# A hybrid decoder step on one core: level products in 32-column parts, pair products by head, the states' decay on ScalarE

## The chip, the cores and the metric

The kernel runs on one core of one Trainium2 chip. The metric is device time in microseconds of one execution. A core has TensorE (PE: matrix products, with weight loads shown as PEld), VectorE (DVE), ScalarE (ACT), GpSimd (POOL) and SyncE (SP, which issues the transfers). They run side by side and wait for each other through semaphores; each takes its own instructions in order.

## What is computed

One layer of a hybrid decoder for two groups: a prompt of 256 new tokens, and 8 samples of 8 tokens each that carry states from before (320 columns of tokens together).

```python
h = rms_norm(x, norm_g)
p = einsum('nld,dp->nlp', h, w_in)                  # 2048 -> 12416 columns
# branch A, RWKV-7: 16 heads of 64
S_t = S_{t-1} diag(w_t) - (S_{t-1} kk_t)(kk_t * a_t)^T + v_t k_t^T;   y_t = S_t r_t
# branch B, HGRN2: 8 heads of 128
S_t = diag(g_t) S_{t-1} + k_t v_t^T;   o_t = S_t^T q_t
merged = sigmoid(ga) * (y_a @ proj_a) + sigmoid(gb) * (o_b @ proj_b)
y = x + merged @ w_out                              # then a final rms_norm
```

The outputs are `y` of both groups, the end states of both branches, and the last projected row. Everything is in float32.

## The kernel before

**Stages.** A start normalises the tokens and turns them. The main loop follows: eight rounds `p`, each with eight projections of 128 columns of `w_in` (r, k, v, za, q, f, i, zb), then `rwkv(p)` for two heads of branch A (stacked on the 128 partitions, 64 each) and `hgrn(p)` for one head of branch B. Four projections of the gate close the loop. The rest (gates, `proj_a`, `proj_b`, `w_out`, the last norm) is untouched by the change.

**Projections.** Values are kept as a high and a low part; a projection is 48 products of 128 x 128 weights with 320 columns (`mps<-hhi,whi`, `mps<-hlo,whi`, `mps<-hhi,wlo`). Weights arrive as 512 KB pieces (`raw`); ScalarE rounds them to `whi`, VectorE takes the difference as `wlo`. There are three buffers of each.

**Order.** `record_all` doesn't issue the loop's instructions; a `Recorder` (`book`) keeps each as an `Op` with its engine, a cost in ns, and the tiles it reads and writes. `link` finds which Op waits for which, `order` simulates the engines and writes out one fixed order for all of them. So every instruction of the loop has the same line, 1396, and is told by its tiles: `a`, `b` and `y` are accumulators (PSUM) of the two branches. On TensorE small products are put between projections; those on a part of the array (a weight of at most 64 columns or rows) are preferred together, since a change of partition is charged, and those of `hgrn` may wait up to `WAIT` = 6000 ns for company. Small products are given a margin of 250 ns after their inputs.

**RWKV of the prompt** goes by four chunks of 64 tokens; block 4 is the samples. `bk2[:, ci]` has two kinds of columns (64 each) with both heads on the partitions, and `arp[:, ci]` holds the two heads apart, with zeros where the other head is, so one product of 128 rows and 256 columns gives both heads' pair products (`a<-arp,bk`, accumulator `pg`), which VectorE masks into `g2`. The chunk chain (`chunks`: `rhs`, `uv`, `st`, `sf`) then runs from chunk to chunk over TensorE, ScalarE and VectorE.

**RWKV of the samples.** The end states are one product per head, `uv` (64 columns) with `bm`, 64 key columns masked for each of the eight samples, 512 columns (`pd2`; tiles `big` and `s0t`). GpSimd makes the masks' products.

**HGRN.** The prompt's attention inside 128 tokens is built in levels. `level(sz)` scales keys and queries for blocks of `sz`, and a product of 128 x 128 keys and queries gives all pairs, of which a mask (`mu8`) keeps the blocks that belong to the level: levels 0 (`k0`, `q0`) and 8 in one bank, 16, 32 and 64 in another, later one. The samples' own pairs are a product of 64 x 64. `pos` multiplies the samples' states with their queries in eight products of 32 columns. The states decay by one multiplication of 1024 columns on GpSimd (`s0`, `dec`), then two products are added.

Of the kernel before, what the change touches and what calls it, by code (L numbers as in the profile page):

```python
# [11 lines left out]
U8 = mybir.dt.uint8  # L12
# [36 lines left out]
class Op:  # L49
    __slots__ = ("eng", "fn", "args", "kw", "cost", "lat", "uses", "mode", "passes", "cols", "stream",  # L50
                 "succ", "npred", "ready", "rank", "block", "margin", "wait", "port", "hold", "dma", "n")
# [17 lines left out]
class Recorder:  # L69
# [3 lines left out]
    def __init__(self, engines, is_big):  # L73
        self.real, self.ops, self.spans, self.is_big = engines, [], {}, is_big
        self.block, self.wait = None, 0
# [9 lines left out]
    def add(self, eng, name, fn, args, kw):  # L85
# [19 lines left out]
        o.block = self.block  # L105
# [5 lines left out]
        if eng == "PE":  # L111
# [13 lines left out]
            o.cost = o.passes * max(load, stream / min(2, 128 // o.mode[1]))  # L125
# [28 lines left out]
    def link(self):  # L154

        writers, readers = {}, {}
        for o in self.ops:
            o.succ, pred = [], {}
            for name, p0, p1, m, wr, psum in o.uses:
# [22 lines left out]
            o.npred = len(pred)  # L182
            for q, data in pred.values():
# [90 lines left out]
def hybrid_step(ctx, tc, x_prompt, x_sample, state_rwkv, state_hgrn, state_shift, norm_g, w_in,  # L274
# [80 lines left out]
    with tc.tile_pool(name="start", bufs=1) as st, \  # L355
# [83 lines left out]
        seq4 = ctile([96, 4], "seq4")  # L439
# [17 lines left out]
        mf = st.tile([64, 3, 64], F32, name="mf")  # L457
        mu8 = ctile([128, 3, 64], "mu8", U8)
        G.memset(mf, 1.0)
        for n, sz in enumerate((8, 8, 16)):  # L460
            if n == 0:
                mfh = mf[:, 0].rearrange("p (b i) -> p b i", i=8)
                keep_ge(mf[:, 0], [[1, 64]], 0, -1)
                keep_ge(mfh, [[-8, 8], [0, 8]], 0, 1)
                keep_ge(mfh, [[8, 8], [0, 8]], 7, -1)
                continue
            lv = mf[:, n].rearrange("p (b two s) -> p b two s", two=2, s=sz)
            nb = 32 // sz
# [3 lines left out]
        for sl in HS:  # L472
            G.tensor_copy(mu8[sl], mf)
# [49 lines left out]
        with tc.manual_schedule(engines={mybir.EngineType.PE, mybir.EngineType.Activation, mybir.EngineType.DVE,  # L523
# [125 lines left out]
            for j in range(3):  # L649
                S.copy(seq4[32 * j:32 * j + 32], seqm[0:32, 0:4])  # L650
# [34 lines left out]
    def ring(pool, tag, shape, bufs, dt, size, clear=False):  # L685
# [12 lines left out]
        if len(shape) == 2:  # L698
# [5 lines left out]
             "w1": 384, "w2": 320, "w3": 320, "ks": 128, "ket": 256}  # L704


    CLEAR = {"uB", "uE", "ys", "rhs", "rhs2", "k3", "vm", "w1", "vt"}
# [51 lines left out]
    def rwkv(p, r, k, vp, za):  # L759
# [87 lines left out]
        for sp in range(4):  # L847
# [6 lines left out]
        bks = at("bks", (128, 2, 64))  # L854
        V.tensor_mul(bks.rearrange("p j (s i) -> p j s i", i=8), bk2[:, 4].rearrange("p j (s i) -> p j s i", i=8),
                     f[:, None, 8:16, None].to_broadcast([128, 2, 8, 8]))
# [11 lines left out]
        for g in range(3):  # L868
            ps = aps("pg")
            n = 2 if g < 2 else 1  # L870
            for c_ in range(n):
                ci = 2 * g + c_
                T.matmul(ps[:, 256 * c_:256 * c_ + 256], bk2[:, ci].rearrange("p j t -> p (j t)"),
                         arp[:, ci].rearrange("p x h t -> p (x h t)"), start=True, stop=True)
            m = mk[:, 0:2] if g < 2 else mk[:, 2:3]
            V.tensor_mul(g2[:, 2 * g:2 * g + n].rearrange("p c x h t -> p (c x) h t"),
                         ps[:, :256 * n].rearrange("p (a h t) -> p a h t", h=2, t=64),
                         m.rearrange("p c x t -> p (c x) t")[:, :, None].to_broadcast([128, 2 * n, 2, 64]))
# [48 lines left out]
        T.transpose(ps[:, :128], bks.rearrange("p j t -> p (j t)"), ident)  # L927
# [105 lines left out]
        def samples():  # L1033
# [14 lines left out]
            T.matmul(ps[:, :128], g2[:, 4, 0].rearrange("p h t -> p (h t)"), uv[:, 4].rearrange("p h v -> p (h v)"), start=False, stop=True)  # L1048
            rhs = at("rhs2", (128, 2, 64))
# [75 lines left out]
    def hgrn(hd, q, k, v, zb):  # L1125
# [43 lines left out]
        G.memset(att, 0.0)  # L1169

        def level(sz, tag):
            half = lambda t_: t_[:, :NP_].rearrange("p (b two s) -> p b two s", two=2, s=sz)
            kq = bt("kq", (128, NP_), tag=tag)
            if sz in (32, 64):

                side = [kq[:, 128 * x:128 * x + 128].rearrange("p (b s) -> p b s", s=sz) for x in range(2)]
            else:
                side = [half(kq)[:, :, x] for x in range(2)]
# [11 lines left out]

        def products(ps, o_, kq, q_):
            for j in range(2):
                tk_ = slice(128 * j, 128 * j + 128)
                T.matmul(ps[:, o_ + 128 * j:o_ + 128 * j + 128], kq[:, tk_], q_[:, tk_], start=True, stop=True)

        def keep(ps, o_, n):
            own = lambda t_, c_: t_.rearrange("p (j c t) -> p j c t", c=2, t=64)[:, :, c_]
            for c_ in range(2):
                sl = HS[c_]
                V.copy_predicated(own(att[sl, :NP_], c_), mu8[sl, None, n].to_broadcast([64, 2, 64]),  # L1200
                                  own(ps[sl, o_:o_ + NP_], c_))

# [375 lines left out]
```

## Time and profile before

| what | us |
|---|---|
| median of 3 runs | 1157.26 (1156.6 to 1157.67) |
| the profiled execution | 1155.96 |
| its span on the core | 1154.3 |
| TensorE busy | 1135.7 |
| VectorE busy | 775.9 |
| ScalarE busy | 669.2 |
| GpSimd busy | 208.0 |

A group of the profile reads: line, engine, operation, written tile <- read tiles, shapes, count | busy time, mean ns of one | idle time before. The mean of a product is its whole passage, which overlaps the next one's; what one costs TensorE is the distance from start to start, read from the timeline (start, duration, instructions). A view of windows gives a stretch's length, then each engine's busy time and count, the granted clock, and the transfers' share.

### The profile page before, as it was taken

How to read it: one execution, taken by the hardware profiler on the slowest of the kernel's cores; microseconds unless marked ns; L12 is line 12 of the kernel's file. 1: busy time of each engine (PE TensorE's matmuls, PEld its weight loads, DVE VectorE, ACT ScalarE, POOL GpSimd, SP SyncE). 2: the span in 40 equal slices, each digit the busy share in tenths (PEclk: the TensorE clock that was granted, in tenths of full speed). 3: DMA queues.
4: the chain of work that ended last, by engine and by line, in shares of the span. 5: the costliest groups of instructions: out<-in, count | busy, mean ns of one | idle time of the engine just before them, and what ended most of it. 6: DMA issues, size and time to landing. Idle time of an engine off the chain costs nothing.

```text
span 1154.3 us, 20774 instructions
## 1 busy us (share of the span) xinstructions
PE 1135.7 (98%) x7816; PEld 1097.9 (95%) x7816; DVE 775.9 (67%) x1634; ACT 669.2 (58%) x1483; POOL 208.0 (18%) x405
## 2 busy tenths in 40 slices
PE   6999999999999999999999999999999999999997
PEld 6999999999999999999999999999999999998886
DVE  8778878877887888878788686544444444436632
ACT  6766766667666667567667667444444444435322
POOL 9432223222311321421321310000000000000000
PEclk9999999999999999999999999999999999999999
DMA  6745435535445435436435434555555555577512
GB/s 180 199 117 127 129 102 136 142 92 132 129 113 146 117 93 150 131 81 169 120 93 162 115 105 132 148 152 153 152 147 148 151 154 151 146 253 254 182 41 91
DMA packets 283096, 159.69 MB, mean 138 GB/s; under 512 B 22893, under 2 KB 273264, under 8 KB 282356
## 3 DMA queue, kind: packets, MB, share of 16 engines
q1 hardware_dynamic: 282996, 158.37, 48.6%
q8 instruction: 61, 1.00, 0.4%
q14 instruction: 39, 0.32, 0.1%
HBM read 148.53 MB, written 9.81 MB: 137 GB/s over the span
## 4 chain that ended last, share of the span: by engine, by line
PE 96%; POOL 2%; DVE 1%; ACT 1%; issue 0%; DMA 0%; ACTq 0%; POOLq 0%
PE mps L1396 41%; PE a L1396 13%; PE mps L338 6%; PE mps L340 6%; PE mps L339 6%; PE b L1396 4%; PE po L1479 3%; PE po L1481 3%; PE po L1480 3%; PE ppb L338 2%; PE ppa L338 2%; PE ppb L340 2%; PE ppa L340 2%; PE ppa L339 2%; PE ppb L339 2%; PE po L1484 1%
## 5 line engine op out<-in xcount | busy, mean ns | idle before, releaser
L1396 PE MATMUL mps<-hhi,wlo 128*128 128x320 f32 x1088 | 344.9, 317 | 0.0
L1396 PE MATMUL mps<-hlo,whi 128*128 128x320 f32 x1088 | 344.7, 317 | 0.0
L1396 PE MATMUL mps<-hhi,whi 128*128 128x320 f32 x1088 | 344.6, 317 | 0.0
L1396 PEld LDWEIGHTS mps<-hlo,whi 128*128 128x128 f32 x1088 | 204.9, 188 | 3.3 <-issue 3.0
L1396 PEld LDWEIGHTS mps<-hhi,wlo 128*128 128x128 f32 x1088 | 205.0, 188 | 2.7 <-issue 2.4
L1396 PEld LDWEIGHTS mps<-hhi,whi 128*128 128x128 f32 x1088 | 205.0, 188 | 0.8 <-issue 0.4
L329 DVE TENSOR_TENSOR wlo<-raw,whi 128x1024 fp32r<-128x1024 f32 x88 | 107.8, 1225 | 125.0 <-ACT whi L328 124.8
L328 ACT CAST whi<-raw 128x1024 fp32r<-128x1024 f32 x88 | 92.3, 1048 | 163.3 <-PE mps L339 104.8
L1396 ACT CAST whi<-raw 128x1024 fp32r<-128x1024 f32 x134 | 140.6, 1049 | 77.2 <-PE mps L1396 75.8
L1396 DVE TENSOR_TENSOR wlo<-raw,whi 128x1024 fp32r<-128x1024 f32 x134 | 167.5, 1250 | 24.4 <-ACT whi L1396 23.1
L339 PE MATMUL mps<-hlo,whi 128*128 128x320 f32 x448 | 138.5, 309 | 0.0
L338 PE MATMUL mps<-hhi,whi 128*128 128x320 f32 x448 | 138.5, 309 | 0.0
L340 PE MATMUL mps<-hhi,wlo 128*128 128x320 f32 x448 | 138.5, 309 | 0.0
L340 PEld LDWEIGHTS mps<-hhi,wlo 128*128 128x128 f32 x448 | 84.1, 188 | 0.0
L338 PEld LDWEIGHTS mps<-hhi,whi 128*128 128x128 f32 x448 | 84.1, 188 | 0.0
L339 PEld LDWEIGHTS mps<-hlo,whi 128*128 128x128 f32 x448 | 84.1, 188 | 0.0
L1468 DVE TENSOR_TENSOR wlo<-raw,whi 128x1024 fp32r<-128x1024 f32 x32 | 38.5, 1222 | 39.1 <-ACT whi L1467 39.0
L1467 ACT CAST whi<-raw 128x1024 fp32r<-128x1024 f32 x32 | 33.1, 1051 | 48.4 <-DMA raw<-in_w_out_dram 22.4
L1479 PE MATMUL po<-whi,mhi 128*128 128x512 f32 x128 | 50.1, 391 | 0.7 <-DVE gbt L1436 0.7
L1481 PE MATMUL po<-wlo,mhi 128*128 128x512 f32 x128 | 50.0, 391 | 0.0
L1480 PE MATMUL po<-whi,mlo 128*128 128x512 f32 x128 | 50.0, 391 | 0.0
L339 PE MATMUL ppb<-ybl,whi 128*128 128x320 f32 x128 | 39.6, 309 | 0.0
(409 smaller groups left out, 2304.0 us busy)
## 6 DMA issues: line engine op xcount, KB each, us to landing
raw<-in_w_in_dram SPq DMA_DIRECT2D x194, 512.0 KB
raw<-in_w_out_dram SPq DMA_DIRECT2D x32, 512.0 KB
raw<-in_proj_a_dram SPq DMA_DIRECT2D x16, 512.0 KB
raw<-in_proj_b_dram SPq DMA_DIRECT2D x16, 512.0 KB
s<-in_state_hgrn_dram SPq DMA_DIRECT2D x8, 512.0 KB
out_dram<-s SPq DMA_DIRECT2D x8, 512.0 KB
s<-in_state_rwkv_dram SPq DMA_DIRECT2D x8, 256.0 KB
out_dram<-s SPq DMA_DIRECT2D x8, 256.0 KB
```

The source lines that it names most:

```text
L328: S.copy(hi[:, ks], raw[:, ks])
L329: sub.tensor_sub(lo[:, ks], raw[:, ks], hi[:, ks].bitcast(F32))
L338: T.matmul(dst, hi[:, q, :], xhi[:, k, :], start=(k == 0), stop=False)
L339: T.matmul(dst, hi[:, q, :], xlo[:, k, :], start=False, stop=False)
L340: T.matmul(dst, lo[:, q, :], xhi[:, k, :], start=False, stop=(k == nk - 1))
L1396: o.fn(*o.args, **o.kw)
L1467: S.copy(hi, raw)
L1468: V.tensor_sub(lo, raw, hi.bitcast(F32))
L1479: T.matmul(pt, h, hi, start=first, stop=False)
L1480: T.matmul(pt, l, hi, start=False, stop=False)
L1481: T.matmul(pt, h, lo, start=False, stop=end)
L1484: T.matmul(pt, h, hi, start=first, stop=False)
```

## The change

Four edits, and what the planner needs for them.

- *Level products in 32-column parts.* All five levels are computed first. Then `pos`, the products of the levels and the samples' own pairs go out as one group: each key block of 32 tokens is a weight of 32 columns and goes to one of four column parts of the array (`tile32`, part g), with the 32 queries of its own block; level 32 with the 32 queries that follow, level 64 with 64. The results stand in one bank: three masked copies gather the first three levels in `attc` (64 columns), ScalarE spreads them into `att`, VectorE copies the rest. `att` is cleared once at the start and no longer by GpSimd in each head. `kq16`, `kq32`, `kq64` take the buffers of `o`, `ket`, `s1` and `ks`.
- *Pair products by head.* For the four prompt blocks each head's 64 rows are multiplied with that head's 128 columns alone: two products of 64 rows per block, on the upper and lower half of the array's rows, into two banks. The sample block stays as it was.
- *The samples' delta-rule states in four 64 by 64 parts.* `bks` is laid out by halves of the samples, `uh` is `uv` with the samples' halves apart, one masked `bm` serves four samples of each half, and four products of 64 rows, 64 weight columns and 256 columns go to the four quarters of the array, into two banks.
- *Decay on ScalarE.* Eight activations of 128 columns with a scale per partition take the place of the GpSimd multiplication.

`side_by_side` marks products as one group; `link` gives all of a group the waits of each and the highest rank, and the cost of a product in a group is divided by the parts that fit.

```diff
@@ Recorder.add
-            o.cost = o.passes * max(load, stream / min(2, 128 // o.mode[1]))
+            side = 128 // o.mode[1] * (128 // o.mode[0] if o.group else 1)
+            o.cost = o.passes * max(max(load, stream) / side, 7) if o.group else o.passes * max(load, stream / min(2, side))
@@ Recorder.link
+        for members in groups.values():
+            own = {o.n for o in members}
+            shared = {}
+            for o in members:
+                for n, (q, data) in preds[o.n].items():
+                    if n not in own:
+                        shared[n] = q, data or shared.get(n, (q, False))[1]
+            for o in members:
+                preds[o.n].update(shared)
...
+        for members in groups.values():
+            top = max(o.rank for o in members)
+            for o in members:
+                o.rank = top
@@ rwkv
-        for g in range(3):
-            ps = aps("pg")
-            n = 2 if g < 2 else 1
-            for c_ in range(n):
-                ci = 2 * g + c_
-                T.matmul(ps[:, 256 * c_:256 * c_ + 256], bk2[:, ci].rearrange("p j t -> p (j t)"),
-                         arp[:, ci].rearrange("p x h t -> p (x h t)"), start=True, stop=True)
...
+        banks = [aps("pg") for _ in HS]
+        side_by_side([((banks[h][:, 128 * ci:128 * ci + 128], bk2[HS[h], ci].rearrange("p j t -> p (j t)"),
+                        arp[HS[h], ci, :, h]), dict(start=True, stop=True)) for ci in range(4) for h in range(2)])
...
@@ samples
+            uh = at("uh", (128, 128), tag="s0t")
+            for a_ in range(2):
+                S.copy(uh[64 * a_ + 32:64 * a_ + 64], uv[64 + 32 * a_:96 + 32 * a_, 4].rearrange("p h v -> p (h v)"))
...
-            pd = aps("pd2")
-            for h in range(2):
-                bm = at("bm", (128, NSEQ, 64), tag=("big", "s0t")[h])
-                G.tensor_mul(bm, bk[:, 4, None, 64 * h:64 * h + 64].to_broadcast([128, NSEQ, 64]),
-                             seqm[:, :, None].to_broadcast([128, NSEQ, 64]))
-                T.matmul(pd[HS[h], :], uv[:, 4, h, :], bm.rearrange("p s k -> p (s k)"), start=True, stop=True)
-            V.tensor_add(s0, s0, pd.rearrange("p (s k) -> p s k", s=NSEQ))
+            bm = at("bm", (128, 4, 128), tag="big")
+            G.tensor_mul(bm, bk[:, 4, None].to_broadcast([128, 4, 128]), seq4[:, :, None].to_broadcast([128, 4, 128]))
+            pds = [aps("pd2") for _ in HS]
+            side_by_side([((pds[a_][HS[h], :256], uh[HS[a_], 64 * h:64 * h + 64], bm[HS[a_], :, 64 * h:64 * h + 64]),
+                           dict(start=True, stop=True)) for h in range(2) for a_ in range(2)])
+            for a_ in range(2):
+                s0h = s0[:, 4 * a_:4 * a_ + 4]
+                V.tensor_add(s0h, s0h, pds[a_][:, :256].rearrange("p (s k) -> p s k", s=4))
@@ hgrn
-        kq8 = level(8, "w2")
-        ps = bps("pg")
-        products(ps, 0, k0, q0)
-        products(ps, 256, kq8, kq8)
-        keep(ps, 0, 0)
-        keep(ps, 256, 1)
+        kq8, kq16, kq32, kq64 = level(8, "w2"), level(16, "o"), level(32, "ket"), level(64, ("s1", "ks"))
...
+        work = [((ps[32 * j:32 * j + 32, 128 * g:128 * g + 128], qz[:, 4 * g + j], s0[:, 4 * g + j]))
+                for g in range(2) for j in range(4)]
+        tile32 = lambda g, c0, a_, b_: work.append((pg[32 * g:32 * g + 32, c0:c0 + b_.shape[-1]], a_, b_))
+        for n, (a_, b_) in enumerate(((k0, q0), (kq8, kq8), (kq16, kq16))):
+            for j in range(2):
+                for g in range(4):
+                    tk_ = slice(128 * j + 32 * g, 128 * j + 32 * g + 32)
+                    tile32(g, 64 * n + 32 * j, a_[:, tk_], b_[:, tk_])
+        for g in range(4):
+            tile32(g, 192, kq32[0][:, 32 * g:32 * g + 32], kq32[1][:, 32 * g:32 * g + 32])
+        for g in range(4):
+            tile32(g, 224, kq64[0][:, 32 * g:32 * g + 32], kq64[1][:, 64 * (g // 2):64 * (g // 2) + 64])
+        for g in range(2):
+            tk_ = slice(NP_ + 32 * g, NP_ + 32 * g + 32)
+            tile32(g, 288, k0[:, tk_], q0[:, tk_])
+        side_by_side([(x_, dict(start=True, stop=True)) for x_ in work])
+        attc = bt("attc", (128, 2, 32))
+        for n in range(3):
+            V.copy_predicated(attc, mu8[:, None, n].to_broadcast([128, 2, 32]),
+                              pg[:, 64 * n:64 * n + 64].rearrange("p (j t) -> p j t", t=32))
...
-        G.tensor_mul(s0, s0, dec[:, :, None].to_broadcast([128, NSEQ, 128]))
+        for si in range(NSEQ):
+            S.activation(s0[:, si], s0[:, si], AF.Copy, scale=dec[:, si:si + 1])
...
-        kq16, kq32, kq64 = level(16, "w3"), level(32, "w2"), level(64, "w1")
-        ps = bps("pl")
-        products(ps, 0, kq16, kq16)
-        T.matmul(ps[:, 256:384], kq32[:, 0:128], kq32[:, 128:256], start=True, stop=True)
-        T.matmul(ps[:, 384:512], kq64[:, 0:128], kq64[:, 128:256], start=True, stop=True)
...
+    def side_by_side(products):
+        book.group = len(book.ops)
+        for args, kw in products:
+            T.matmul(*args, **kw)
+        book.group = None
```

How the order moves. First TensorE in the first head, where the HGRN products stand (`w_0_...` are the buffers of `kq` and of `k0`, `q0`; `big`, `s0t` those of `bm`, and after the change `s0t` that of `uh`). Before:

```order
L1396 MATMUL b_520<-w_0_525,w_0_517 128x128 x2
...
L1396 MATMUL b_519<-s_0_516,qz 32x128 x8
L1396 MATMUL a_485<-big_514,uv_492 64x512
L1396 MATMUL a_485<-s0t_494,uv_492 64x512
L1396 MATMUL mps<-hlo,whi 128x320
...
L1396 MATMUL b_520<-w_0_525 128x128 x2
L1396 MATMUL b_519<-vm_532,k_0_530 128x512
L1396 MATMUL b_520<-w_0_524 128x128
L1396 MATMUL b_520<-w_0_517 128x128
```

After:

```order
L1435 MATMUL b_522<-s_0_519,qz 32x128 x8
L1435 MATMUL b_523<-w_0_528,w_0_520 32x32 x8
L1435 MATMUL b_523<-w_0_527 32x32 x8
L1435 MATMUL b_523<-o_530 32x32 x8
L1435 MATMUL b_523<-ket_531 32x32 x4
L1435 MATMUL b_523<-ks_533,s_0_532 32x64 x4
L1435 MATMUL b_523<-w_0_528,w_0_520 32x32 x2
L1435 MATMUL mps<-hlo,whi 128x320
...
L1435 MATMUL a_486<-big_517,s0t_497 64x256
L1435 MATMUL a_487<-big_517,s0t_497 64x256
```

The level products, which stood at two places apart from `pos`, stand right behind it in one piece; the states' products, which touched `pos`, follow later behind projections (in this head; over the eight heads the two touch in five before and in three after).

Then the decay of the samples' states in the same head (`s_0_...` with `dec`). Before, on GpSimd:

```order
L1396 TENSOR_TENSOR vm_532<-v_0_521,seq_165 96x512
L1396 TENSOR_TENSOR fd_513<-id_146,fq_512 128x256
L1396 COPY ys_499<-id_144 64x64
L1396 TENSOR_TENSOR vm_532<-v_0_521,seq_165 96x512
L1396 TENSOR_TENSOR s_0_516<-s_0_516,dec_528 128x1024
```

After, on ScalarE:

```order
L1435 ACTIVATE s_0_519<-s_0_519,dec_535 128x128 x2
L1435 CAST k_0_537<-b_523 32x128 x4
L1435 ACTIVATE w_0_528<-R_526 128x128
L1435 ACTIVATE w_0_520<-R_526 128x128
L1435 ACTIVATE uv_495<-a_488 64x64
L1435 ACTIVATE s_0_519<-s_0_519,dec_535 128x128 x4
L1435 COPY att_529<-attc_536 32x2x32 x3
L1435 COPY o_530<-b_522 128x64
...
L1435 ACTIVATE sf_513<-st_512,f_493 128x128
L1435 ACTIVATE dl_539<-F_525 128x1
L1435 COPY rhs_507<-a_486 64x64
```

The last four decays and the copies into `att` stand on ScalarE between the chunk chain's `uv` and its next `sf` and `rhs`, which queue behind them.

More of the change, by code (lines that the diff above doesn't have):

```diff
@@ L50 @@
     __slots__ = ("eng", "fn", "args", "kw", "cost", "lat", "uses", "mode", "passes", "cols", "stream",
-                 "succ", "npred", "ready", "rank", "block", "margin", "wait", "port", "hold", "dma", "n")
+                 "succ", "npred", "ready", "rank", "block", "margin", "wait", "port", "hold", "dma", "n", "group")
 def span_of(ap):
@@ L74, in __init__ @@
         self.real, self.ops, self.spans, self.is_big = engines, [], {}, is_big
-        self.block, self.wait = None, 0
+        self.block, self.wait, self.group = None, 0, None
     def proxy(self, eng):
@@ L181, in link @@
             pred.pop(o.n, None)
-            o.npred = len(pred)
-            for q, data in pred.values():
+        groups = {}
+        for o in self.ops:
+            if o.group is not None:
+                groups.setdefault(o.group, []).append(o)
+        for members in groups.values():
[7 more added lines that the diff above has]
+                preds[o.n].update(shared)
+        for o in self.ops:
+            o.npred = len(preds[o.n])
+            for q, data in preds[o.n].values():
                 q.succ.append((o, data))
@@ L648, in hybrid_step @@
             fetch(2, 1024, 1)
-            for j in range(3):
+            for j in range(4):
                 S.copy(seq4[32 * j:32 * j + 32], seqm[0:32, 0:4])
@@ L703, in hybrid_step @@
     SIZES = {"uK": 384, "uS": 384, "uE": 384, "uA": 320, "uB": 384, "uQ": 320, "big": 512, "s0t": 512, "v": 384,
-             "w1": 384, "w2": 320, "w3": 320, "ks": 128, "ket": 256}
-    CLEAR = {"uB", "uE", "ys", "rhs", "rhs2", "k3", "vm", "w1", "vt"}
+             "w1": 384, "w2": 320, "w3": 320, "ks": 128, "ket": 256, "o": NT}
+    CLEAR = {"uB", "uE", "ys", "rhs", "rhs2", "k3", "vm", "w1", "vt", "att", "attc"}
     def at(name, shape=(128, NT), tag=None, bufs=1, dt=F32):
@@ L1168, in hgrn @@
         att = bt("att", (128, 2 * 128 + 64))
-        G.memset(att, 0.0)
         def level(sz, tag):
             half = lambda t_: t_[:, :NP_].rearrange("p (b two s) -> p b two s", two=2, s=sz)
-            kq = bt("kq", (128, NP_), tag=tag)
             if sz in (32, 64):
-                side = [kq[:, 128 * x:128 * x + 128].rearrange("p (b s) -> p b s", s=sz) for x in range(2)]
+                half_ = bt("kq", (128, NP_), tag=tag) if sz == 32 else None
+                kq = [half_[:, 128 * x:128 * x + 128] for x in range(2)] if sz == 32 else \
+                    [bt("kq", (128, 128), tag=t_) for t_ in tag]
+                side = [x.rearrange("p (b s) -> p b s", s=sz) for x in kq]
             else:
+                kq = bt("kq", (128, NP_), tag=tag)
                 side = [half(kq)[:, :, x] for x in range(2)]
@@ L1220, in hgrn @@
         ps = bps("pos")
-        for si in range(NSEQ):
-            j = si % 4
-            T.matmul(ps[32 * j:32 * j + 32, 128 * (si // 4):128 * (si // 4) + 128], qz[:, si, :], s0[:, si, :],
-                     start=True, stop=True)
+        pg = bps("pg")
+        work = [((ps[32 * j:32 * j + 32, 128 * g:128 * g + 128], qz[:, 4 * g + j], s0[:, 4 * g + j]))
[8 more added lines that the diff above has]
+            tile32(g, 192, kq32[0][:, 32 * g:32 * g + 32], kq32[1][:, 32 * g:32 * g + 32])
+        for g in range(4):
+            tile32(g, 224, kq64[0][:, 32 * g:32 * g + 32], kq64[1][:, 64 * (g // 2):64 * (g // 2) + 64])
[7 more added lines that the diff above has]
+                              pg[:, 64 * n:64 * n + 64].rearrange("p (j t) -> p j t", t=32))
+        for g in range(4):
+            own = slice(32 * g, 32 * g + 32)
+            S.copy(att[own, :NP_].rearrange("p (j t) -> p j t", j=2)[:, :, own], attc[own])
+            if g < 2:
+                V.copy_predicated(att[own, NP_ + 32 * g:NP_ + 32 * g + 32], mu8[own, 0], pg[own, 288:320])
+        for j in range(2):
+            for b in range(2):
+                V.tensor_copy(att[64 * b:64 * b + 32, 128 * j + 64 * b + 32:128 * j + 64 * b + 64],
+                              pg[64 * j + 32 * b:64 * j + 32 * b + 32, 192:224])
+            V.tensor_copy(att[0:64, 128 * j + 64:128 * j + 128], pg[HS[j], 224:288])
         sot = bt("sot", (128, 256), tag="ket")
@@ L1227, in hgrn @@
         ps = bps("pke")
-        T.matmul(ps[:, 128:192], k0[:, NP_:], q0[:, NP_:], start=True, stop=True)
         T.transpose(ps[0:64, :128], es[:, 1], ident)
-        V.copy_predicated(att[0:64, NP_:], mu8[0:64, 0], ps[0:64, 128:192])
         k3 = bt("k3", (128, 2, 128), dt=F32R)
```

66 lines of the change are left out of this document (29 added, 37 removed).

## The prediction

> **What bounds the kernel now.** First the page: span, busy shares, and the chain that ended last, by engine.
>
> ```profile
> span 1154.3 us, 20774 instructions
> PE 1135.7 (98%) x7816; PEld 1097.9 (95%) x7816; DVE 775.9 (67%) x1634; ACT 669.2 (58%) x1483; POOL 208.0 (18%) x405
> PE 96%; POOL 2%; DVE 1%; ACT 1%; issue 0%; DMA 0%; ACTq 0%; POOLq 0%
> ```
>
> TensorE carries the chain. A share over the whole span says nothing of the stage that changes, so next come two stretches: one of projections alone, and the loop over the heads, which holds every changed line. Last, from the waits, what ScalarE waits for longest in that loop.
>
> ```profile
> core 0: us, PE busy (x) PEld busy (x) DVE busy (x) ACT busy (x) POOL busy (x), PEclk, DMA share, GB/s
> 800.00:900.00 100.00, 100.00 (x684) 100.00 (x683) 43.32 (x50) 44.66 (x67) 0.00 (x0) 1.00 0.54 152
> 29.00:698.00 669.00, 667.98 (x4897) 652.58 (x4897) 543.34 (x1332) 451.43 (x1148) 180.81 (x349) 1.00 0.46 126
> ...
> ACT whi L1396 <- PE mps L1396: 75.8, 79, 2.1
> ```
>
> A projection product of 320 columns costs 100/684 = 0.146 us. In the loop TensorE stands for only 669.00 − 667.98 = 1.02 us, at a granted clock of 1.00; VectorE is busy 81%, ScalarE 67%, and ScalarE waits for TensorE to free weight buffers. The others run ahead of TensorE, so the change is worth what it takes out of TensorE's stream, less any time that TensorE newly stands.
>
> **What a pass costs.** Each fp32 product shows as two matmul records, which I call passes. The timeline of TensorE in the first head (start, duration, what) gives three prices.
>
> ```profile
> 90.09 0.60 PE L1396 MATMUL b<-w,w 128*128 128x128 f32 x4
> 90.54 0.61 PE L1396 MATMUL a<-pp,uB 128*128 128x128 f32 x4
> ...
> 93.56 0.33 PE L1396 MATMUL b<-w,w 128*128 128x64 f32 x2
> 93.73 0.27 PE L1396 MATMUL b<-ident,es 128*64 128x128 f32 x1
> ```
>
> Four passes of 128 columns take 90.54 − 90.09 = 0.45 us, 0.112 each; two passes of 64 columns take 0.17.
>
> ```profile
> 62.84 2.32 PE L1396 MATMUL a<-arp,bk 128*128 128x256 f32 x10
> 64.81 0.50 PE L1396 MATMUL mps<-hhi,whi 128*128 128x320 f32 x1
> 65.14 0.31 PE L1396 MATMUL mps<-hlo,whi 128*128 128x320 f32 x1
> ```
>
> The pair products: ten passes of 256 columns and one projection from 62.84 to 65.14, so (2.30 − 0.15)/10 = 0.215 a pass, or 0.84 ns a column.
>
> ```profile
> 100.51 0.31 PE L1396 MATMUL mps<-hhi,whi 128*128 128x320 f32 x1
> 100.75 0.64 PE L1396 MATMUL b<-s,qz 128*32 128x128 f32 x16
> 101.32 0.64 PE L1396 MATMUL a<-big,uv 128*64 128x512 f32 x1
> 101.33 0.64 PE L1396 MATMUL a<-s0t,uv 128*64 128x512 f32 x1
> 101.80 0.59 PE L1396 MATMUL a<-big,uv 128*64 128x512 f32 x1
> 101.81 0.59 PE L1396 MATMUL a<-s0t,uv 128*64 128x512 f32 x1
> 102.33 0.42 PE L1396 MATMUL mps<-hlo,whi 128*128 128x320 f32 x1
> ...
> 101.32 0.13 PEld L1396 LDWEIGHTS a<-big,uv 128*64 128x64 f32 x1 [0.20 <-DVE F L1396]
> 101.38 0.14 PEld L1396 LDWEIGHTS a<-big,uv 128*64 128x64 f32 x1
> ```
>
> Here the array already works in parts: sixteen passes of HGRN on four 32-column parts, then the RWKV states on two 64-column parts. Sixteen passes one by one would take 16 x 0.112 = 1.79 us; they take 101.32 − 100.75 = 0.57, four rounds of 128 columns (0.43) and a margin, so the four parts do run at once. The same rows price a change of the array's partition. In: 100.75 − 100.51 − 0.15 = 0.09. Out: 102.33 − 101.80 less 512 columns (0.43) = 0.10. And the second pass starts 0.48 − 0.43 = 0.05 late, which is the weight load of 64 columns (101.38 − 101.32): 0.03 for 32 columns, 0.11 for 128.
>
> **The change part by part, per head.**
>
> *Level products out.* The counts of the groups are
>
> ```profile
> L1396 PE MATMUL b<-w 128*128 128x128 f32 x96 | 16.1, 276 | 0.0
> L1396 PE MATMUL b<-w,w 128*128 128x128 f32 x32 | 4.9, 274 | 0.0
> L1396 PE MATMUL b<-w,w 128*128 128x64 f32 x16 | 2.6, 247 | 0.0
> ```
>
> that is (96 + 32)/8 = 16 passes of 128 columns and 2 of 64: 16 x 0.112 + 0.17 = −1.96 us.
>
> *Level products in.* 34 products on 32-column parts, 68 passes, issued right behind HGRN's sixteen: 48 + 8 + 4 passes of 32 columns and 8 of 64. Four parts at once make 12 + 2 + 2 rounds of 32 columns (the sample's last four use two parts) and 2 rounds of 64. A round of 32 columns streams in 0.027 and loads its weights in 0.027 beside the round before: 16 x 0.028 + 2 x 0.055 = 0.56 us. No row shows a pass so short. From below, two passes on different parts start 0.01 apart (101.32, 101.33), rows too coarse to promise less than 0.45. From above, the sixteen passes follow each other at (0.57 − 0.10)/16 = 0.029 on average, and nothing in the trace is quicker over a stretch: 68 x 0.029 = 1.97. I take 0.56: the sixteen are fully explained by their 128 columns, so 0.029 is their stream's price and not the issue's.
>
> A sentence of the Trainium skill speaks for the upper end: "TensorE: Matmul & The Clock Gate", section "Wait — 56ns, not 53.3ns?", says that starts never come closer than about 25 ns however few columns stream. By it the 68 passes would be an estimated 1.7 us. The rows at 101.80 and 101.81 break it for one pair on different parts; that it is broken by 68 in a row no run here shows.
>
> *Samples' delta-rule states.* Two products of 512 columns on two parts become four of 256 on four (64 by 64). Bounds: all four at once, 2 rounds of 0.215 = 0.43; or the halves that contract over different rows one after another, 0.86. No row shows two such row halves at once. I take 0.43, nearest to the column parts, which run at once.
>
> Old stretch as a whole: 102.33 − 100.51 − 0.15 = 1.67. New: the level group 0.09 + 0.03 + 0.43 + 0.56 + 0.10 = 1.21; the states 0.09 + 0.05 + 0.43 + 0.10 = 0.67; sum 1.88. In TensorE's order old pieces touch in 5 heads of 8 and new ones in 3; apart costs one way out and in more than the step between, about 0.09. That makes 1.70 before and 1.85 after: +0.15.
>
> *Pair products by head.* Four blocks out, 8 passes of 0.215 = −1.72. In: 16 passes of 128 columns in two row halves. Side by side 8 x 0.108 + in 0.09 + first load 0.11 + out 0.10 = +1.16; one after another +2.02. I take the first, for the reason above: −0.56 net.
>
> *Other engines.* Their rows:
>
> ```profile
> L1396 ACT ACTIVATE sf<-st,f 128x128 f32<-128x128 f32 x24 | 9.6, 401 | 1.8 <-DVE st L1396 1.7
> L1396 ACT CAST k<-b 32x128 fp32r<-32x128 f32 x32 | 8.1, 255 | 2.1 <-DVE att L1396 1.7
> L1396 ACT COPY uE<-uB 64x64 f32<-64x64 f32 x16 | 3.9, 245 | 0.2
> L1396 DVE COPY_PREDICATED att<-mu,b 64x128 f32<-64x128 uint8 x48 | 14.3, 299 | 2.3 <-PE b L1396 1.2
> L1396 DVE COPY_PREDICATED att<-mu,b 64x64 f32<-64x64 uint8 x8 | 1.8, 221 | 0.5 <-PE b L1396 0.4
> L1396 DVE TENSOR_TENSOR s<-s,a 128x512 f32<-128x512 f32 x16 | 11.0, 686 | 3.0 <-PE a L1396 1.6 <-ACT ket L1396 1.0
> L1396 DVE TENSOR_TENSOR g<-a,mk 128x256 f32<-128x256 f32 x8 | 3.3, 414 | 0.0
> L1396 POOL TENSOR_TENSOR s<-s,dec 128x1024 f32<-128x1024 f32 x8 | 15.6, 1948 | 3.6 <-PE b L1396 3.2 <-issue 0.3
> L1396 POOL TENSOR_TENSOR s0t<-bk,seqm 128x512 f32<-128x512 f32 x8 | 8.3, 1042 | 123.5 <-PE a L1396 123.5
> ```
>
> ScalarE gains eight decays (8 x 0.401), four copies of 32 x 128 (4 x 0.255) and four of 32 x 64 (at most 4 x 0.245): +5.2 us a head, 451 to 493 us of some 650, 76%. VectorE: six masked copies of 0.299 and one of 0.221 become five of at most 0.221 (−0.9), and one addition of 0.686 becomes two of 0.414 (+0.1): it stays near 82%. GpSimd drops the decay and one of two masks, 3.0 us (and a clearing of a tile). All of this lies beside TensorE: it costs nothing while ScalarE stays ahead, and 5.2 x 8 = 42 us at most if it does not. TensorE works in order, though, and its level group now waits for all five levels at once, with projections queued behind. The planner puts it where its costs expect the inputs, as before; I double the 1.02 us that TensorE stands today: +1.0 for the loop.
>
> **Sum.** −1.96 + 0.15 − 0.56 = −2.37 a head, x 8 = −19.0, +1.0 = −18.0 us. The profiled execution took 1155.96 (its span and 1.7 around it), which gives 1138.0; the median of the runs lies 1.3 above it, so **1139 us**.
>
> **The rivals.**
>
> *A. Issue, not columns, sets the pace of the 68 passes.* For it: nothing in the trace is quicker than 0.029 over a stretch. Against it: four streams explain that. Price 1.97 − 0.56 = 1.41 a head: 1139 + 11.3 = 1150. It is the mechanism of the skill's 25 ns; that figure by itself would give an estimated 1148.
>
> *B. Row halves run one after another.* For it: no row shows two at once. Against it: column parts do. Price 2.02 − 1.16 for the pairs and 0.43 for the states, 1.29 a head: 1139 + 10.3 = 1149. A and B together: 1161, slower than before.
>
> *C. ScalarE's decays hold up the chunk chain.* In ScalarE's order four decays (1.60 us) stand ahead of `sf` and `rhs`, on which TensorE's next chunk products wait, and projections queue behind those. Were both fours of a head (3.2 us) to pass to TensorE, 25.7 us: 1165, slower. It decides from 18/8 = 2.25 us a head. Against it: TensorE has projections ahead of each chunk product, and today's order leaves it standing 1.02 us in all.
>
> That the parts are not issued together can't be: the order shows them in a row.
>
> **How the numbers follow.** My forecast 0.62, with a range of its own from 1135 to 1143; A 0.12; B 0.11; A and B 0.04; C 0.07; something smaller that ends within 0.2% (2.3 us, about what a measurement of this kernel can tell from no change) 0.04. Faster: 0.62 + 0.12 + 0.11 = 0.85; same 0.04; slower 0.04 + 0.07 = 0.11. The range runs from 1134 (passes at 0.01 or less, no new standing, and one way in or out cheaper) to 1152, past A and B; it leaves out the slower cases and those near no change.
>
> **What would show it.** Level group: 84 passes in about 1.1 us from first start to the next projection; near 2.5 is A. Pair products: pairs starting together, about 0.1 a pair, 1.2 us in all; one start each 0.1 is B. States: two rounds of 0.22. TensorE's stand in the loop near 2 us; ten or more, with waits on ScalarE, is C. ScalarE near 76%. I am wrong if the loop ends other than 16 to 21 us earlier, or if the projections behind it change.

## The result, and the profile after

| | before | after |
|---|---|---|
| median (lowest to highest) | 1157.47 us (1156.6 to 1158.74) | 1139.96 us (1139.87 to 1140.02) |
| the profiled execution, its span | 1155.96, 1154.3 | 1139.92, 1138.2 |

The ratio is 0.9848 (0.9831 to 0.9865): 17.5 us faster by the medians, 16.0 by the two profiled executions; the one profiled of before was its quickest. The forecast was 1139 us. The page of the changed kernel, its loop as a stretch (length, then each engine's busy time and count, the clock, the transfers), and ScalarE's longest wait in the loop:

```profile
span 1138.2 us, 21837 instructions
PE 1122.0 (99%) x8312; PEld 1087.7 (96%) x8312; DVE 766.8 (67%) x1634; ACT 700.7 (62%) x1612; POOL 179.8 (16%) x385
PE 98%; DVE 1%; POOL 0%; ACT 0%; issue 0%; ACTq 0%; DVEq 0%; POOLq 0%
```

```profile
29.00:681.00 652.00, 651.61 (x5393) 639.36 (x5393) 531.08 (x1331) 480.38 (x1269) 153.45 (x328) 1.00 0.47 129
...
ACT whi L1435 <- PE mps L1435: 65.4, 57, 3.7
```

TensorE still carries the chain, now 98% of it. ScalarE is at 480.38/652.00 = 74%, VectorE at 81%, and ScalarE still waits for TensorE to free weight buffers, so the other engines are still ahead. From the first recorded projection to the first projection behind the loop it was 689.1 us and is 672.1: the change lies in the loop. Of these 17.0 us, 0.8 is a stand at 37 us that only before has. Against it the loop of after begins 1.0 later, at 30.1 us instead of 29.1, and the profiled executions differ by 16.0. What follows the loop takes 436.0 in both.

Three pieces of TensorE's timeline of after (start, duration, instructions) answer the prediction's three: the level group in the first head, a pair block, and the states.

```profile
102.68 0.31 PE L1435 MATMUL mps<-hhi,wlo 128*128 128x320 f32 x1
102.83 0.38 PE L1435 MATMUL a<-g,uv 128*128 128x128 f32 x2
103.14 0.65 PE L1435 MATMUL b<-s,qz 128*32 128x128 f32 x16
103.60 0.31 PE L1435 MATMUL b<-w,w 128*32 128x32 f32 x16
...
104.18 0.24 PE L1435 MATMUL b<-w,w 128*32 128x32 f32 x4
104.35 0.41 PE L1435 MATMUL mps<-hhi,whi 128*128 128x320 f32 x1
```

The 84 passes take 104.35 − 103.14 = 1.21 us. The first sixteen take 103.60 − 103.14 = 0.46, as said. Between 103.60 and 104.18 stand 64 passes: 0.58/64 = 9 ns each.

```profile
63.01 0.31 PE L1435 MATMUL mps<-hhi,wlo 128*128 128x320 f32 x1
63.24 1.16 PE L1435 MATMUL a<-arp,bk 64*128 64x128 f32 x16
64.34 0.41 PE L1435 MATMUL mps<-hhi,whi 128*128 128x320 f32 x1
64.59 0.31 PE L1435 MATMUL mps<-hlo,whi 128*128 128x320 f32 x1
64.74 0.59 PE L1435 MATMUL a<-arp,bk 128*128 128x256 f32 x2
...
106.11 0.31 PE L1435 MATMUL mps<-hhi,whi 128*128 128x320 f32 x1
106.35 0.66 PE L1435 MATMUL a<-big,s0t 64*64 64x256 f32 x8
106.94 0.41 PE L1435 MATMUL mps<-hlo,whi 128*128 128x320 f32 x1
107.19 0.31 PE L1435 MATMUL mps<-hhi,wlo 128*128 128x320 f32 x1
```

Sixteen pair passes take 64.34 − 63.24 = 1.10 and 63.24 − 63.01 − 0.15 = 0.08 for the way in: row halves run at once. The states take 106.94 − 106.35 = 0.59: four quarters run at once. Something stands here that the rows of before did not make plain: behind a return to the whole array the *second* projection is late too (64.59 − 64.34 = 0.25 and 107.19 − 106.94 = 0.25 instead of 0.15), then it is over (64.74 − 64.59 = 0.15).

### The profile page after: what moved, and what is told of

The parts are those of the page before. It is cut to its first block, busy times and chain, and to the rows that moved or that the text cites. A ratio compares the mean times of both kernels' runs of the same rounds, so it can differ in the third digit from the quotient of the medians.

```text
span 1138.2 us, 21837 instructions
## 1 busy us (share of the span) xinstructions
PE 1122.0 (99%) x8312; PEld 1087.7 (96%) x8312; DVE 766.8 (67%) x1634; ACT 700.7 (62%) x1612; POOL 179.8 (16%) x385
## 3 DMA queue, kind: packets, MB, share of 16 engines
q8 instruction: 65, 1.06, 0.4%
## 4 chain that ended last, share of the span: by engine, by line
PE 98%; DVE 1%; POOL 0%; ACT 0%; issue 0%; ACTq 0%; DVEq 0%; POOLq 0%
PE mps L1435 42%; PE a L1435 12%; PE mps L359 6%; PE mps L360 6%; PE mps L361 6%; PE b L1435 3%; PE po L1518 3%; PE po L1519 3%; PE po L1520 3%; PE ppb L359 2%; PE ppa L359 2%; PE ppb L360 2%; PE ppa L360 2%; PE ppb L361 2%; PE ppa L361 2%; PE po L1524 1%
## 5 line engine op out<-in xcount | busy, mean ns | idle before, releaser
L1435 DVE TENSOR_TENSOR wlo<-raw,whi 128x1024 fp32r<-128x1024 f32 x134 | 166.6, 1243 | 18.1 <-ACT whi L1435 16.7
L359 PE MATMUL ppa<-yah,whi 128*128 128x320 f32 x128 | 39.6, 309 | 0.0
```

The costliest lines, as they stand in the source:

```text
L359: T.matmul(dst, hi[:, q, :], xhi[:, k, :], start=(k == 0), stop=False)
L1435: o.fn(*o.args, **o.kw)
```

## How the comparisons below are counted

A share of busy time hides short stands, because a product's own passage (0.31 us for a projection) lasts longer than the distance to the next one (0.15). So I summed starts: for each pass of TensorE in the loop, the distance to the next start. Passes on a part of the array are summed as *blocks* (but for two products a head with the identity on 64 columns, the same in every kernel). Every other pass is given the median distance of its kind between the same two kinds of neighbours, over the profiles of all kernels here (*other work*). What a pass took over that by more than 0.02 us is a *stand*. A stand of 0.7 to 0.9 us in some profiles at 37 us, the loop's start, is left out: it appears where the loop began 0.9 us earlier, and the two cancel.

| kernel | median us | blocks | other work | stands |
|---|---|---|---|---|
| before | 1157.2 to 1157.5 | 12.7 | 674.7 | 2.6 |
| levels_only | 1147.30 | 18.1 | 658.9 | 3.8 |
| levels_pair | 1142.67 | 26.9 | 646.8 | 2.3 |
| no_pair | 1140.63 | 14.4 | 659.3 | 0.4 |
| no_states | 1141.97 | 26.5 | 646.8 | 2.2 |
| no_decay | 1139.40 | 23.5 | 647.2 | 2.5 |
| after | 1139.96 | 23.2 | 647.2 | 3.2 |
| gpsimd_costs | 1137.06 | 23.2 | 647.0 | 0.4 |
| decay_back_joined | 1140.01 | 23.6 | 646.6 | 3.5 |
| halves_in_line | 1144.02 | 27.6 | 647.1 | 2.9 |
| two_more_changes | 1147.25 | 26.0 | 650.2 | 3.9 |
| double_levels | 1149.53 | 32.3 | 647.1 | 3.2 |

Blocks and other work together are the *stream*, which the four edits are meant to shorten: 687.4 before, 670.4 after, −17.0. Stands depend on the fixed order, which the planner writes anew for every kernel.

My theory after the result: the stream adds up edit by edit, and the stands are what the planner's order happens to leave. Rivals: the edits interact; or the pace of the level passes has another limit (fetch of instructions, ScalarE) that is near.

## Undoing one edit

**Pair products back to four products of 256 columns.**

```diff
-        banks = [aps("pg") for _ in HS]
-        side_by_side([... for ci in range(4) for h in range(2)])
+        for g in range(3):
+            ps = aps("pg")      # two blocks to a bank, 256 columns each, as before
```

> The changed kernel with the pair products by head undone (one product of 128 rows and 256 columns per block again). Theory T, TensorE's stream is the only thing that counts: the block costs 8 passes of 0.215 = 1.72 us again in place of the 1.18 that the trace of the change shows (0.09 in, 0.89 for the passes, 0.20 to the next projection) and of a second projection that starts 0.105 late; +0.44 us a head, +3.5 in all: 1143.5 (1142.5 to 1144.5). Rival D, the gain comes from what VectorE and GpSimd were relieved of (masked copies, masks, decay), since VectorE's work on the pair products is the same in both: within 1 us of 1140.

Measured 1140.63 us (1140.25 to 1141.12), ratio to before 0.9856 (0.9839 to 0.9872): only 0.7 slower than after, where 3.5 was expected. The stream is longer by what was said: blocks −8.8, other work +12.1, together +3.3. But in this order TensorE stands 0.4 us instead of 3.2. The edit's worth and the order's luck can't be told apart by the clock alone, so I measured the edit a second time, below.

**States back to two products of 512 columns.**

```diff
-            side_by_side([((pds[a_][HS[h], :256], uh[HS[a_], 64 * h:64 * h + 64], bm[HS[a_], :, 64 * h:64 * h + 64]), ...
+                T.matmul(pd[HS[h], :], uv[:, 4, h, :], bm.rearrange("p s k -> p (s k)"), start=True, stop=True)
```

> The changed kernel with the samples' delta-rule states undone (two products of 512 columns on two column parts, two masks on GpSimd, one addition). T: from the first start to the next projection 1.01 us (trace of before) in place of 0.59, +0.42 a head = +3.4; the order leaves level group and states touching in 5 heads in place of 3, -0.2 each: 1143.0 (1142 to 1144). Rival D: GpSimd has one mask of 1.04 us a head more on the port it shares with VectorE, ScalarE four copies less: no statement on TensorE, up to +8.3 us, 1148, if the mask counts in full.

Measured 1141.97 (1141.81 to 1142.01), ratio 0.9868 (0.9853 to 0.9883): +2.0. Stream +2.9, as the theory has it; stands 1.0 less.

**Decay back on GpSimd.**

```diff
-        for si in range(NSEQ):
-            S.activation(s0[:, si], s0[:, si], AF.Copy, scale=dec[:, si:si + 1])
+        G.tensor_mul(s0, s0, dec[:, :, None].to_broadcast([128, NSEQ, 128]))
```

> The changed kernel with the decay of the samples' HGRN states back on GpSimd (one multiplication of 1.95 us a head) in place of eight activations of 0.40 on ScalarE. T: nothing on TensorE's stream moves, 1140.0 (1139.4 to 1140.6). Rival D (GpSimd's work held VectorE back, and so the whole): slower, up to 15.6 us. Rival C (ScalarE's queue, longer by 3.2 us a head, holds TensorE's chunk products): faster by more than 1 us.

Measured 1139.40 (1139.25 to 1139.66), ratio 0.9846 (0.9832 to 0.9861): 0.6 faster than after by the medians, at the edge of what was said. The decay on ScalarE brings nothing; GpSimd has room for it.

**All three undone: the level products alone.**

> The changed kernel with pair products, states and decay all undone: the level products alone. T: the edits add up, 1140.0 + 3.5 + 3.4 - 0.4 (touching in 5 heads in place of 3) = 1146.5 (1145.5 to 1147.5), that is -1.3 us a head against the kernel before: 1.96 of level passes out, 0.64 in. Rival D: most of the gain gone with the relief of GpSimd, 1152 or more.

Measured 1147.30 (1147.19 to 1147.39), ratio 0.9914 (0.99 to 0.9929). This is in the range of T, and rival D (1152 or more) is out. The level products alone bring 10 us of the 17.3 (against the 1157.28 of before in this round), in the stream 10.4.

**Pair products added to that.**

```diff
# levels_only, and again
+        side_by_side([((banks[h][:, 128 * ci:128 * ci + 128], bk2[HS[h], ci]..., arp[HS[h], ci, :, h]), ...
```

> The change with its states and its decay as before, so the pair products by head are added to the level products alone, where 'levels_only' took 1147.3. Theory (the stream adds, the standing is a matter of the fixed order): the eight pair blocks, with their ways in and out, take 3.3 us less of TensorE's stream than ten passes of 256 columns each, and the standing falls anywhere between the 0.6 and 3.8 us that the orders so far had, against 3.8 in 'levels_only': 1144.0, between 1141 and 1144.3. Rival (the edit is worth what its single undoing showed, 0.7 us): 1146.6.

Measured 1142.67 (1142.37 to 1142.71), ratio 0.9873 (0.986 to 0.9887). Against the level products alone −4.6: stream −3.3, the same as in the first comparison to a tenth, and stands 1.5 fewer. The same edit moved the time by 0.7 in one place and 4.6 in the other, and its stream by 3.3 in both. The rival that it is worth 0.7 is out.

So the stream adds up: −10.4 levels, −3.3 pairs, −2.9 states, −0.3 decay, sum −16.9, against −17.0 measured whole. The decay isn't TensorE's work, so its 0.3 shows how exact this count is.

## Testing the prices

**The halves of the pair products in line**, all four blocks of one half first, then the other.

```diff
-        ... for ci in range(4) for h in range(2)])
+        ... for h in range(2) for ci in range(4)])
```

> The changed kernel with the pair products in another order: all four blocks of the upper row half, then all four of the lower, in place of the halves in turn. If TensorE starts passes in the program's order, the lower half waits for the upper: 16 x 0.108 + the same ways in and out, +0.84 us a head, +6.7: 1147. If it looks far enough ahead in its queue to fill both halves: 1140.2 (the states touch in one head less, +0.2). The sixteen passes of HGRN's states, whose two passes per product stand in a row in the program, start four at a time, so some looking ahead there is; eight passes deep no run has shown. I take 1147 with 0.6.

Measured 1144.02 (1143.84 to 1144.06), ratio 0.9886 (0.9871 to 0.9901): +4.1, between the two. Its timeline:

```profile
63.24 1.71 PE L1435 MATMUL a<-arp,bk 64*128 64x128 f32 x16
64.88 0.41 PE L1435 MATMUL mps<-hhi,whi 128*128 128x320 f32 x1
65.13 0.31 PE L1435 MATMUL mps<-hlo,whi 128*128 128x320 f32 x1
```

1.64 us a block instead of 1.10, in all eight blocks. In the records of single passes the first start 0.21 and then 0.11 apart; then the second half's first weight load comes up, its first pass starts beside the fifth (0.006 behind), and the halves overlap until the first has run out; five passes of the second then stand alone. So TensorE reaches some four passes ahead, and not sixteen: parts run at once only where the order puts them next to each other, which is why the two orders of the same products differ by 0.54 us a block.

**A change of partition twice more in each head.** A product of 32 columns, whose result nobody reads, is set among products on the whole array at two places.

```diff
             T.transpose(pv[:, 128 * w:128 * w + 128], vp[:, 128 * w:128 * w + 128], ident)
+        side_by_side([((pv[0:32, 384:416], id32, id32), dict(start=True, stop=True))])
```

> The changed kernel with two more changes of the array's partition per head: a product of 32 rows' worth of columns (32 x 32, on one column part, its result read by nobody) alone between projections. Each is two passes of 0.027. By the prices of the prediction (in 0.09, first load 0.03, out 0.10): 0.27, x 16 = 4.3 us, 1144.3. By what the trace of the change adds (after every way out the second projection starts 0.105 late as well): 0.38 x 16 = 6.0, 1146.0.

Measured 1147.25 (1146.74 to 1147.53), ratio 0.9913 (0.9896 to 0.9929): +7.3, more than either. Sixteen more changes lengthen the stream by 2.8 + 3.0 = 5.8, that is 0.36 each. One of them:

```profile
231.13 0.31 PE L1437 MATMUL mps<-hhi,wlo 128*128 128x320 f32 x1
231.37 0.25 PE L1437 MATMUL a<-id 128*32 128x32 f32 x2
231.55 0.41 PE L1437 MATMUL mps<-hhi,whi 128*128 128x320 f32 x1
231.80 0.31 PE L1437 MATMUL mps<-hlo,whi 128*128 128x320 f32 x1
```

The two small passes take 231.55 − 231.37 = 0.18 until the next start, the way in 231.37 − 231.13 − 0.15 = 0.09, and the second projection behind is 231.80 − 231.55 − 0.15 = 0.10 late. The prediction's prices had no such last term. The other 0.7 to 1.5 are stands.

**The level passes twice**: the same 68 products again in the same group, with the same results.

```diff
-        side_by_side([(x_, dict(start=True, stop=True)) for x_ in work])
+        side_by_side([(x_, dict(start=True, stop=True)) for x_ in work + work[8:]])
```

> The changed kernel with the 34 level products issued twice in their group (the second 68 passes write the same values again; work is added, not left out). In the trace of the change the first 24 level passes start 0.0079 us apart on average (fours of 0.007 and a step), the later ones 0.0083 to 0.009, two every 0.0166. T, the pace stays where it settled: 60 x 0.009 + 8 x 0.0166 = 0.67 us a head, +5.4, less 0.2 since the states touch in one head more: 1145.2 (1144.4 to 1146.2). Rival, the early pace came from a queue filled ahead and falls further once it is empty, to 0.029 at worst: up to +15.8, 1156. Rival, columns alone bind (0.007 a pass): +0.53 a head, 1144.0.

Measured 1149.53 (1149.0 to 1149.77), ratio 0.9933 (0.9919 to 0.9948): +9.6 where 5.2 was expected. The blocks are 9.1 us longer: 5.1 of it is the pace, 0.64 us a head, 3.7 are three stands inside the group, each in another head, and 0.3 is a stand inside one block of the states. Its timeline, and stretches behind it (the clock is the third number from the end):

```profile
348.63 0.19 PE L1435 MATMUL b<-w,w 128*32 128x32 f32 x1
351.04 0.25 PE L1435 MATMUL b<-w,w 128*32 128x32 f32 x3 [2.20 <-issue]
```

```profile
348.60:351.00 2.40, 0.24 (x23) 0.09 (x9) 0.17 (x1) 1.14 (x5) 0.00 (x0) 1.00 0.32 88
...
351.90:352.80 0.90, 0.90 (x7) 0.82 (x5) 0.87 (x6) 0.04 (x1) 0.00 (x0) 0.50 0.09 26
352.80:355.10 2.30, 2.30 (x11) 2.30 (x11) 1.19 (x7) 2.20 (x9) 0.00 (x0) 0.50 0.01 4
355.10:357.00 1.90, 1.90 (x14) 1.85 (x14) 1.09 (x3) 1.15 (x5) 0.57 (x1) 0.97 0.03 9
```

Three passes before its end the group stops for 2.20 us with nothing that the profile shows to wait for, and then the granted clock is 0.50 for some 3 us, in which projections start 0.27 apart. The two other stands inside the group are 0.82 and 0.35 us. A transfer of the queue that carries instructions begins at 348.5 and takes 1.06 us, so the sequencer running dry is likely for the long stand; but no such transfer lies at the second one, and nothing I ran tells this apart. It stays open. In the changed kernel, with half as many passes, no group stops.

The Trainium skill, "TensorE: Matmul & The Clock Gate", section "What's actually happening", puts the step down to half clock behind an idle window of about 3.4 us. Here the only stand ahead of it was one of 2.20 us; it happened once in these runs.

**ScalarE's decays three times**: two more activations by ones ahead of each, 51 us in all.

```diff
-            S.activation(s0[:, si], s0[:, si], AF.Copy, scale=dec[:, si:si + 1])
+            for k_ in range(3):
+                S.activation(s0[:, si], s0[:, si], AF.Copy, scale=dec[:, si:si + 1] if k_ == 2 else rs_a[:, 1:2])
```

> The changed kernel with every decay preceded by two activations that multiply by one: 16 more of 0.40 us a head on ScalarE, 51 us in all; ScalarE goes from 74% to 81% of the loop. T: ScalarE lies beside TensorE and still runs ahead: 1139.5 to 1141. Rival C, ScalarE's queue holds TensorE's chunk products: from a fourth of it, 13 us, to all, 51 us: 1153 to 1191.

Measured 1142.48 (1141.76 to 1143.54), ratio 0.9874 (0.9859 to 0.9889): 51 us more on ScalarE cost 2.5, more than T's range had. The loop's end, in the experiment and in after:

```profile
29.00:691.00 662.00, 661.45 (x5467) 650.51 (x5467) 537.63 (x1329) 517.89 (x1395) 151.16 (x328) 1.00 0.47 129
691.00:706.00 15.00, 14.55 (x98) 13.36 (x97) 8.41 (x16) 12.43 (x32) 0.00 (x0) 1.00 0.48 129
```

```profile
691.00:706.00 15.00, 15.00 (x104) 15.00 (x103) 12.50 (x17) 12.57 (x22) 0.00 (x0) 1.00 0.51 146
```

Up to 691 TensorE stands 0.55 us in 662 although ScalarE is at 78%. Behind 691, where the last head has no further projections to hide behind, it stands 0.45 us in 15, and VectorE's last result of the loop starts at 709.8 instead of 695.2. By starts TensorE stands 3.2 us from 693 to 720, where after loses none. The changed kernel is far from ScalarE's bound, so rival C is out.

## Testing the stands

The changed kernel stands 3.2 us. One of its places, from the timelines of GpSimd and TensorE:

```profile
468.76 2.12 POOL L1435 TENSOR_TENSOR yz<-g,id 64x128 f32<-64x128 f32 x2 [2.94 <-DVE g L1435]
470.95 1.24 POOL L1435 TENSOR_TENSOR yz<-id,yz 64x128 f32<-64x128 f32 x2
...
471.71 0.31 PE L1435 MATMUL mps<-hhi,whi 128*128 128x320 f32 x1
471.86 0.31 PE L1435 MATMUL mps<-hlo,whi 128*128 128x320 f32 x1
472.25 0.72 PE L1435 MATMUL a<-yz,uE 128*128 128x128 f32 x4
```

`yz` ends at 470.95 + 1.24 = 472.19 and TensorE's product starts at 472.25, 0.24 late (472.25 − 471.86 − 0.15), with projections queued behind it. The planner prices a GpSimd operation at 200 ns and 1.66 a column, 412 for these; they take 620 to 1060 here, and a product of four columns (`arp`) 648 on average, where the planner has 207. So the order puts the product too early.

**GpSimd's prices as the trace shows them**, nothing else.

```diff
-  ... else 200 + free * 1.66
+  ... else 330 + free * 0.4 if "copy" in name else 560 + free * 1.15
```

> The change, with GpSimd's prices in the order's simulation set to what the trace shows (two tiles: 560 ns and 1.15 a column, copies 330 and 0.4, where all had 200 and 1.66). Theory: TensorE's 3.15 us of standing in the changed kernel come from inputs that the order expects earlier than GpSimd has them (yz, arz, arp); with right prices the standing falls to 1 to 2 us, and the states and the level group touch in four heads instead of three (0.3 less): 1138.2, between 1137.3 and 1139.3. Rival (the standing is made by other delays, or falls as it happens to fall): 1139.4 to 1142.

Measured 1137.06 (1136.66 to 1137.25), ratio 0.9826 (0.9812 to 0.9839): 2.9 us faster than the change, a little below the range expected, and the fastest kernel here. Its stream is that of after within 0.2; the stands fall from 3.2 to 0.4. The same place:

```profile
469.70 1.98 POOL L1435 TENSOR_TENSOR yz<-g,id 64x128 f32<-64x128 f32 x2 [5.07 <-DVE g L1435]
...
472.07 1.11 POOL L1435 TENSOR_TENSOR yz<-id,yz 64x128 f32<-64x128 f32 x2
...
473.45 0.31 PE L1435 MATMUL mps<-hlo,whi 128*128 128x320 f32 x1
473.60 0.31 PE L1435 MATMUL mps<-hhi,wlo 128*128 128x320 f32 x1
473.75 0.62 PE L1435 MATMUL a<-yz,uE 128*128 128x128 f32 x4
```

GpSimd is no quicker: `yz` ends at 473.18. But the product now stands behind projections until 473.75, and no time is lost.

**Decay back on GpSimd, and the states' products waiting for company**, so that they touch the level group in five heads instead of three.

```diff
+            book.wait = book.WAIT
             side_by_side([((pds[a_][HS[h], :256], ...
+            book.wait = 0
```

> The change with the decay back on GpSimd (alone 1139.4) and the states' products allowed to wait for company as HGRN's are, so that they touch the level group in five heads instead of three. Theory: two entries and two ways out less, 0.3 each, and a standing like that of the decay alone: 1138.8, between 1137.8 and 1139.4. Rival (what the wait delays, the states' additions and the end of the loop, costs more): above 1139.6.

Measured 1140.01 (1139.88 to 1140.11), ratio 0.9851 (0.9837 to 0.9864). The stream is 0.5 shorter than without the wait (670.2 against 670.7), as said; the order stands 1.0 more, so that the time is 0.6 above that of the decay alone, where the rival had it. A gain of the size of a stand can't be planned for in this kernel.

**The same with GpSimd's prices.**

> The last two edits together: decay on GpSimd, states that wait for company (here they touch in four heads), and GpSimd's prices as the trace shows them. Theory: 1139.4 less 0.3 for one touch more and 1 to 2 of standing: 1137.6, between 1136.8 and 1138.6, the fastest of all. Rival (the standing falls as it happens to fall): 1139 to 1142.

Measured 1141.02 (1140.89 to 1142.39), ratio 0.9862 (0.9849 to 0.9876), slower than either alone. Up to 693 us TensorE is never idle, and stands 1.6 us by starts. Then, from the stretches behind the last head and its waits (engine, line, what it waited for, us, times, longest):

```profile
700.00:706.00 6.00, 6.00 (x42) 5.77 (x41) 1.91 (x4) 5.33 (x11) 0.00 (x0) 1.00 0.41 110
706.00:712.00 6.00, 4.72 (x29) 3.97 (x28) 5.54 (x8) 3.90 (x7) 0.00 (x0) 1.00 0.57 166
...
PE mps L359 <- ACT whi L349: 1.0, 1, 1.0
PE mps L361 <- DVE wlo L350: 0.2, 1, 0.2
```

TensorE is idle for 1.28 us because the weights of the next stage are late: this order ends the last head later (VectorE's last result of the loop starts at 708.6, without the new prices at 699.3), and the work for it falls where the next stage's weights are to be rounded: ScalarE is busy for 5.33 us of the first 6.00, VectorE for 5.54 of the second. Up to 693 us the stands fell here too, from 3.5 to 1.6. Behind it they are 2.7 by starts, where the kernel without the new prices has none; that loss is one that the planner, which ends with the loop, doesn't price. So the same prices were worth 2.9 us beside one order of the work and cost 1.0 beside another.

## Why the prediction was right

The forecast of 1139 against 1139.96, −18.3 against −17.5 by the medians, −18.0 against −16.0 on the profiled executions. Part of the closeness is luck: on the profiled executions the forecast was 1138.0 against 1139.92, and the 1.3 us that it added for the median made up for most of that, but after's median lies only 0.04 above its profiled execution. The loop ends 16.0 us earlier (702.2 instead of 718.2), just inside the 16 to 21 that the prediction gave as its sign. By its steps:

- **TensorE bounds the loop, and the change is worth what leaves its stream.** Right: −17.0 of the loop is stream.
- **Level products out, −1.96 a head.** Right: between before and `levels_only` the other work falls by 674.7 − 658.9 = 15.8, 1.97 a head.
- **Level passes in, 0.56.** The right mechanism at a price a little low: `double_levels` gives 0.64, so the pace is neither the four streams' alone (0.56) nor anything near rival A's 1.97. Of what A names there is a trace: 9 ns a pass where the streams alone would take 8. The timeline above has 64 passes in 0.58 us. So the 25 ns between starts of the Trainium skill ("TensorE: Matmul & The Clock Gate", section "Wait — 56ns, not 53.3ns?"), which the prediction set beside it, do not hold across column parts.
- **Pair products, −0.56 a head.** The block itself came as worked out: in 0.08 and 1.10, together 1.18 against 1.16. Removed work was 13.8 against 13.8. Yet the edit brought 3.3 in the stream where 4.5 was forecast. The term that failed is the way out: "out 0.10" is only the first projection's part, and the second starts 0.10 to 0.11 late as well, 0.8 us over the eight blocks. Some 0.3 lies in the blocks and their edges. The halves do run at once, so rival B is out.
- **States, 0.67.** The timeline has 0.09 + 0.59 = 0.68, and the blocks fell by 3.3. The stream gained 2.9, since 0.4 went into other work. Half of that is the late second projection, which was never charged: TensorE returns to the whole array 21 times in after and 19 times in `no_states`, 0.10 each.
- **TensorE's standing double, +1.0.** Wrong as a measure. The idle view fell, from 1.02 to 0.39 over the two stretches shown (0.60 of the 1.02 is the stand at 37 us), while the starts show 2.6 and 3.2 us of standing without that one. Idle time doesn't see a stand that is shorter than a passage. That the loss was small was right. Much of it went when GpSimd's prices were put right, which the prediction did not look at: 3.2 to 0.4 in one order, 3.5 to 1.6 up to 693 us in another. But `no_pair` stands 0.4 with the old prices, so an order can also get there by chance.
- **Other engines cost nothing.** Right to within 1 us: `no_decay` is 0.6 faster than after, and 51 us more on ScalarE in `more_act` cost 2.5.

In the sum, the stream brought 2 us less than the −19.0 of the prediction: the levels −10.4 where its terms give −11.2, the pairs −3.3 instead of −4.5, the states −2.9 instead of −3.3, and the decay 0.3 the other way. The stands grew by 0.6 instead of 1.0.

## What to carry to other kernels

Price a change of the array's partition whole: here the way in, the way out and the late second product behind it are about 0.3 us, so small products on parts of the array pay only in groups, and parts run at once only where they stand within a few passes of each other in the order. Where an order is planned by prices, measure a kernel's stands by distances from start to start and check the prices of the engine that is late; correcting GpSimd's prices was worth 2.9 us here, as much as a whole edit, though beside another order it cost 1.0, at the loop's end where the planner doesn't look. And where every build has its own order, judge an edit by its stream in two surroundings: the same pair products moved the time by 0.7 and by 4.6 us.

## What the runs showed of the hardware

- Passes of 32 columns on four column parts start 9 ns apart over 64 passes, at a granted clock of 1.00.
- Behind a return to the whole array not only the first but also the second projection is late, by 0.10 us (0.25 instead of 0.15 from start to start).
- Row halves of 64 x 128 (16 passes of 128 columns in 1.10 us) and quarters of 64 x 64 (8 passes of 256 columns in 0.59) run at once in float32. A pass some four places ahead in the order starts early, one eight places ahead doesn't: 1.64 us instead of 1.10 with the halves in line.
- In a doubled group 149 passes in 1.7 us ended once in a stand of 2.20 us with no wait to be seen, and a granted clock of 0.50 for some 3 us after it.
